# Three input projections of a decoder trunk: one 512-column pass for the high and the low part of 256 weight columns

## The chip, the cores and the metric

The kernel runs on one core of a Trainium2 chip. The metric is the device time of one execution in microseconds, from the first to the last instruction and what lies around them; lower is better.

## What is computed

A causal decoder of four layers on 512 tokens of 1024 features, float32. Each layer adds a token mixer and then a conv-gated MLP, each behind an RMS norm:

```python
for i in range(4):
    h = rms_norm(x, norm_mix[i])
    y = (dilated_attention, mla_attention, diff_attention, swa_sink_attention)[i](h, ...)
    x = x + y
    x = x + conv_ffn(rms_norm(x, norm_ffn[i]), ...)
```

Mixers 0, 2 and 3 begin with a projection of h onto 9*512, 3*1024 and 1280 columns. The columns give queries, keys and values; queries and keys are RMS-normed per head of 64 columns, the values are used as they are. Mixer 1 goes through two low-rank latents instead.

## The kernel before

**Precision.** Each float32 operand of the large products is split into a high part, rounded to the fp32r type of TensorE, and a low part, the rest. `mm3` (L304) makes a product of three matmuls: high by high, high by low, low by high. All three go into the same accumulator in PSUM.

**Layout.** The state is feature-major: `xh[k]`, `xl[k]` are the high and low part of features 128k to 128k+127, as 128 x 512 tokens. The projections of mixers 0, 2 and 3 are token-major: `tok` (L808) holds 128 tokens of `xh` or `xl` in the array (the weight load) and streams 256 columns of the projection's weights past them (the matmul). One call makes two token blocks c0 and c0+1, which share one PSUM bank of 512 columns, over k = 0 to 7: per k and block three loads and three matmuls of 256 columns.

**Units.** 256 weight columns are a unit: two weight tiles of 1024 columns (k 0 to 3, k 4 to 7), two calls of `tok`. Mixer 0 has 18 units (`ORDER0`), mixer 2 has 12, mixer 3 has 5. Behind each `tok` a task is spawned: `qk_post`, `q_post`, `kv_post` (squares, mean, normalising by `head_norm`, L831, all of which read the bank) or `v_post` (scaling by the row's norm factor). The bank is given back (`drop`, L828) when the task has read it. The tasks wait until the norm factor `self.rs` is known.

**Weights.** `wload` (L247 on) brings a tile from HBM into a ring of three, `_wsplit` (L233) makes the parts: ACT writes `wh` (L239), DVE writes `wl` (L242) of it. The parts stand in rings of three tiles each (`WB`, L67). `freew` (L265) gives a pair back; only then can the next item be split into it. In `tok` the first of a unit's two pairs goes back when the second call has used k = 3, so three quarters through the unit.

**Order.** The tasks are generators, of which each `round` (L123) runs one step. `tok` calls `round` once per k. The heads' work (logits, softmax, transposes, products with the values) is interleaved with the projections in this way. The instructions' order on each engine is then settled when the program is built, by a planner that goes by this order and by its own estimate of durations (`schedule_with_timeline_sim=True` in the launch lines); on the chip each engine runs its own list in order. PSUM has eight banks: three "a", two "lg", two "tr", one "av"; the projections use "a", and `self.early` (L976) lets the fourth and fifth call of a mixer use "lg".

Of the kernel before, what the change touches and what calls it, by code (L numbers as in the profile page):

```python
# [19 lines left out]
KD = 8  # L20
# [46 lines left out]
WB = 3  # L67
# [28 lines left out]
class Builder:  # L96
    def __init__(self, ctx, tc, ap, plan):
# [15 lines left out]
        self.ring(self.main, "wh", [128, WMAX], F32R, WB)  # L113
        self.ring(self.main, "wl", [128, WMAX], F32R, WB)
# [93 lines left out]
    def wpump(self):  # L208
        again = True
        while again:  # L210
# [13 lines left out]
            while self.wnext < len(self.witems) and self.free("wh") and self.free("wl"):  # L224
# [4 lines left out]
                wh, wl = self.now("wh"), self.now("wl")  # L229
                self.wsplit.append((wh, wl))  # L230
                self.spawn(self._wsplit(i, wh, wl))
# [33 lines left out]
    def freew(self):  # L265
        self.give("wh", "wl")
        self.wpump()
# [559 lines left out]

    def drop(self, bank):  # L828
        self.give(self.banks.pop(id(bank))[1])
# [144 lines left out]
    def mixer_rings(self, **more):  # L974
        mp = self.mp
        self.early = 5  # L976
# [21 lines left out]
    def mixer2(self):  # L998
# [8 lines left out]
        def qk_post(bank, c0, nt, h):  # L1007
            while self.rs is None:
                yield
            yield from self.head_norm([bank[:, i * 256:(i + 1) * 256] for i in range(2)],  # L1010
                                      [nt[:, c0 + i] for i in range(2)], 64,
                                      [self.e2[:, c0 + i:c0 + i + 1] for i in range(2)])
            self.drop(bank)
# [13 lines left out]
        def v_post(bank, c0, v, j):  # L1027
            while self.rs is None:
                yield
            for i in range(2):  # L1030
                nc.scalar.activation(v[:, c0 + i], bank[:, i * 256:(i + 1) * 256], AF.Copy,
                                     scale=self.rs[:, c0 + i:c0 + i + 1])
            self.drop(bank)
# [95 lines left out]
    def mixer0(self):  # L1129
# [11 lines left out]
        def qk_post(bank, c0, nt, p, g):  # L1141
            while self.rs is None:
                yield
            yield from self.head_norm([bank[:, i * 256:(i + 1) * 256] for i in range(2)],
                                      [nt[:, c0 + i] for i in range(2)], 64,
                                      [self.e2[:, c0 + i:c0 + i + 1] for i in range(2)])
            self.drop(bank)
# [16 lines left out]
        def v_post(bank, c0, v, store, key):  # L1164
            while self.rs is None:
                yield
            for i in range(2):
                nc.scalar.activation(v[:, c0 + i], bank[:, i * 256:(i + 1) * 256], AF.Copy,
                                     scale=self.rs[:, c0 + i:c0 + i + 1])
            self.drop(bank)  # L1170
# [149 lines left out]
        for p in range(4):  # L1320
            for t in ORDER0[p]:
                ws = [self.getw(), self.getw()]
                if t in (0, 1, 3):
                    x, g = self.now("nt"), (1, 2, None, 0)[t]
                    post = lambda b, c0: qk_post(b, c0, x, p, g)
                else:
                    y = self.now("v" if t == 4 else "vn")
                    post = lambda b, c0: v_post(b, c0, y, v0 if t == 4 else v12, p // 2 if t == 4 else p)
                for c0 in (0, 2):
                    b = self.tok(ws, 256, c0, self.xsrc, range(KD), done=c0 == 2)  # L1330
                    self.spawn(post(b, c0))
# [18 lines left out]
    def mixer1(self):  # L1350
        nc, mp = self.nc, self.mp
        self.mixer_rings(v=([128, 4, 256], F32, 2), nt=([128, 4, 384], F32, 2), p=([128, 512], F32, 10),
# [267 lines left out]
    def mixer3(self):  # L1620
# [9 lines left out]
        def kv_post(bank, c0, nt):  # L1630
            while self.rs is None:
                yield
            v = lambda i: bank[:, i * 256 + 128:(i + 1) * 256]
            for i in range(2):
                nc.scalar.activation(vh[:, c0 + i], v(i), AF.Copy, scale=self.rs[:, c0 + i:c0 + i + 1])
            yield from self.head_norm([bank[:, i * 256:i * 256 + 128] for i in range(2)],
                                      [nt[:, c0 + i, :128] for i in range(2)], 64,
# [297 lines left out]
```

## Time and profile before

| what | value |
|---|---|
| median of three runs | 2376.08 us (2373.54 to 2377.24) |
| the profiled execution | 2377.44 us |
| its span, first to last instruction | 2375.5 us |
| mean granted TensorE clock, share of full speed | 0.992 |
| TensorE busy | 98% of the span |
| DVE, ACT busy | 75%, 54% |

Busy times of TensorE are modelled to the end of each pipelined matmul, so neighbouring matmuls overlap in the records: a matmul of 256 columns shows as 283 to 289 ns, but the next begins 120 ns later. The time that a matmul takes is therefore read from a run of them in the chain of waits (length by count), not from its own duration.

### The profile page before, as it was taken

The numbers are of one execution on the slowest core, as the hardware profiler recorded it, in microseconds if no ns is written. First come the engines' busy times: TensorE is split into PE (matmuls) and PEld (weight loads), VectorE is DVE, ScalarE is ACT, GpSimd is POOL, SyncE is SP. The second block draws the span as 40 slices with busy tenths as digits, with TensorE's granted clock in tenths as the row PEclk, the third lists the DMA queues.
The fourth block names the chain that finished last, engine by engine and source line by source line (L and its number), as shares of the span: only waits on it lengthen the run. The fifth ranks groups of instructions, "written<-read, shape, count | busy, mean of one in ns | idle before, by whom it ended". The sixth has DMA issues, their size and how long they took to land.

```text
span 2375.5 us, 41007 instructions
## 1 busy us (share of the span) xinstructions
PE 2328.8 (98%) x16116; PEld 2116.3 (89%) x16116; DVE 1773.8 (75%) x3152; ACT 1279.8 (54%) x2378; POOL 310.6 (13%) x242
## 2 busy tenths in 40 slices
PE   8999989999999999999999999899999999999999
PEld 8999969999997777999989998799999977899998
DVE  6565688787768749877786776888787676987776
ACT  5565555544557746544554564554445575544443
POOL 0000022222002102212100000122220000222210
PEclk9999999999999999999999999899999999999999
DMA  5233255554231115655435554565542533655632
GB/s 182 82 99 90 90 138 166 150 150 136 76 104 45 34 58 153 176 151 152 123 93 153 147 143 130 145 164 152 149 138 74 144 101 93 176 161 152 160 107 89
DMA packets 98160, 298.43 MB, mean 126 GB/s; under 512 B 12144, under 2 KB 18480, under 8 KB 97968
## 3 DMA queue, kind: packets, MB, share of 16 engines
q1 hardware_dynamic: 85296, 249.67, 33.0%
q0 software_dynamic: 12672, 46.14, 11.0%
q8 instruction: 127, 2.08, 0.4%
q14 instruction: 65, 0.53, 0.1%
HBM read 273.62 MB, written 4.32 MB: 117 GB/s over the span
## 4 chain that ended last, share of the span: by engine, by line
PE 95%; DVE 3%; ACT 1%; issue 1%; DMA 0%; SPq 0%; DVEq 0%; ACTq 0%
PE a L302 51%; PE tr L302 19%; PE lg L302 17%; PE av L302 3%; PE tr L969 2%; PE tr L863 2%; DVE r L628 0%; DVE wl L242 0%; ACT p L284 0%; DVE p L909 0%; ACT wh L239 0%; DVE x L452 0%; DVE acc L466 0%; DMA x<-in_x_dram 0%; PE lg L1288 0%
## 5 line engine op out<-in xcount | busy, mean ns | idle before, releaser
L239 ACT ACTIVATE wh<-wraw 128x1024 fp32r<-128x1024 f32 (+3 forms) x357 | 357.8, 1007 | 486.6 <-PE a L302 214.8
L242 DVE TENSOR_TENSOR wl<-wraw,wh 128x1024 fp32r<-128x1024 f32 (+3 forms) x357 | 446.6, 1253 | 139.9 <-ACT wh L239 138.7
L302 PE MATMUL a<-wh,xh 128*128 128x256 f32 (+1 forms) x1088 | 313.7, 289 | 6.3 <-ACT xh L456 6.3
L302 PE MATMUL a<-wl,xh 128*128 128x256 f32 (+1 forms) x1088 | 311.4, 286 | 0.0
L302 PE MATMUL a<-wh,xl 128*128 128x256 f32 (+1 forms) x1088 | 310.4, 286 | 0.0
L302 PE MATMUL a<-ch,wh 128*128 128x256 f32 x960 | 271.6, 283 | 0.0
L302 PE MATMUL a<-cl,wh 128*128 128x256 f32 x960 | 271.5, 283 | 0.0
L302 PE MATMUL a<-ch,wl 128*128 128x256 f32 x960 | 271.4, 283 | 0.0
L302 PE MATMUL tr<-hl,wh 128*128 128x512 f32 x656 | 256.2, 390 | 0.0
L302 PE MATMUL tr<-hh,wh 128*128 128x512 f32 x656 | 255.6, 392 | 0.0
L302 PE MATMUL tr<-hh,wl 128*128 128x512 f32 x656 | 250.4, 390 | 0.0
L256 POOL DMA_DIRECT2D fraw<-in_wup_dram x80 | 69.4, 870 | 1182.3 <-DMA fraw<-in_wup_dram 591.2
L302 PEld LDWEIGHTS a<-wh,xh 128*128 128x128 f32 x1088 | 208.7, 192 | 9.4 <-ACT xh L456 6.3
L302 PEld LDWEIGHTS a<-wl,xh 128*128 128x128 f32 x1088 | 208.9, 192 | 2.1 <-issue 0.9
L302 PEld LDWEIGHTS a<-wh,xl 128*128 128x128 f32 x1088 | 208.0, 192 | 2.3 <-issue 1.1
L302 PE MATMUL a<-xh,wh 128*128 128x256 f32 (+1 forms) x704 | 206.6, 293 | 2.3 <-ACT wh L239 2.3
L302 PE MATMUL a<-xh,wl 128*128 128x256 f32 (+1 forms) x704 | 206.0, 293 | 0.0
L302 PE MATMUL a<-xl,wh 128*128 128x256 f32 (+1 forms) x704 | 205.1, 293 | 0.0
L302 PEld LDWEIGHTS a<-cl,wh 128*128 128x128 f32 x960 | 183.9, 192 | 1.4
L302 PEld LDWEIGHTS a<-ch,wh 128*128 128x128 f32 x960 | 183.8, 191 | 1.4
L302 PEld LDWEIGHTS a<-ch,wl 128*128 128x128 f32 x960 | 183.9, 192 | 0.0
L302 PEld LDWEIGHTS tr<-hh,wl 128*128 128x128 f32 x656 | 123.3, 188 | 25.1
(274 smaller groups left out, 5879.3 us busy)
## 6 DMA issues: line engine op xcount, KB each, us to landing
wraw<-in_wup_dram SPq DMA_DIRECT2D x136, 512.0 KB, 3.3
fraw<-in_wup_dram SPq DMA_DIRECT2D x80, 512.0 KB, 3.4
fraw<-in_wup_dram POOLq DMA_DIRECT2D x80, 512.0 KB, 5.8
wraw<-in_w_dram SPq DMA_DIRECT2D x69, 512.0 KB, 3.5
wraw<-in_wd_dram SPq DMA_DIRECT2D x64, 512.0 KB, 3.3
wraw<-in_wd_dram SPq DMA_DIRECT2D x32, 384.0 KB, 3.1
wraw<-in_o_dram SPq DMA_DIRECT2D x24, 384.0 KB, 3.3
sk<-qh SPq DMA_DIRECT2D x68, 128.0 KB, 2.4
```

The lines of the kernel that those rows point to most:

```text
L239: nc.scalar.activation(wh[:, sl], raw[:, sl], AF.Copy)
L242: nc.vector.tensor_tensor(wl[:, sl], raw[:, sl], wh[:, sl].bitcast(F32), op=OP.subtract)
L256: self.nc.gpsimd.dma_start(out=s["tile"][:, :s["n"]], in_=s["plus"], accum_op=OP.add)
L302: self.nc.tensor.matmul(out, a, b, start=start, stop=stop, skip_group_check=True)
L863: self.nc.tensor.transpose(b[:rows, o * 128:(o + 1) * 128], src(c), self.mirror if query else self.ident)
L969: nc.tensor.transpose(b[:, j * 128:(j + 1) * 128], blk, self.mirror)
```

## The change

`tok` is replaced, in mixers 0, 2 and 3, by `tok_wide`. A weight item is now one tile of two halves, high and low. One token block c at a time: per k one matmul of 512 columns, `xh` by high and low half side by side, into the two halves of a bank, and one of 256 columns, `xl` by the high half, added into the first half. The two halves are added outside PSUM by a new task `gather`: ACT copies the second half into the SBUF tile, DVE adds the first half to it, and the bank is given back. The later tasks read and overwrite the SBUF tile. `round` is called for every second k. The first weight tile of a unit goes back in the fourth block, seven eighths through the unit.

```diff
-        self.ring(self.main, "wh", [128, WMAX], F32R, WB)
-        self.ring(self.main, "wl", [128, WMAX], F32R, WB)
+        self.ring(self.main, "ww", [128, 2, WMAX], F32R, WB)
...
+    def tok_wide(self, ws, x, post):
+        per = KD // len(ws)
+        n = []
+
+        def gather(bank, out):
+            self.nc.scalar.activation(out, bank[:, 256:], AF.Copy)
+            yield
+            self.nc.vector.tensor_tensor(out, bank[:, :256], out, op=OP.add)
+            self.give("a")
+            n.append(out)
+
+        def then(c0):
+            while len(n) < c0 + 2:
+                yield
+            yield from post(c0)
+        for c in range(4):
+            out = self.now("a")
+            sl = slice(c * 128, (c + 1) * 128)
+            for k in range(KD):
+                w = ws[k // per][2][:, :, k % per * 256:k % per * 256 + 256]
+                a = self.xsrc(k)
+                self.mm(out.rearrange("p (i d) -> p i d", i=2), a[0][:, sl], w, k == 0)
+                self.mm(out[:, :256], a[1][:, sl], w[:, 0], False, k == KD - 1)
+                if c == 3 and (k + 1) % per == 0:
+                    self.freew()
+                if k % 2:
+                    self.round()
+            self.spawn(gather(out, x[:, c]))
+            if c % 2:
+                self.spawn(then(c - 1))
...
     def mixer_rings(self, **more):
         mp = self.mp
-        self.early = 5
...
-        def v_post(bank, c0, v, j):
+        def v_post(c0, v, j):
             while self.rs is None:
                 yield
             for i in range(2):
-                nc.scalar.activation(v[:, c0 + i], bank[:, i * 256:(i + 1) * 256], AF.Copy,
-                                     scale=self.rs[:, c0 + i:c0 + i + 1])
-            self.drop(bank)
+                nc.scalar.activation(v[:, c0 + i], v[:, c0 + i], AF.Copy, scale=self.rs[:, c0 + i:c0 + i + 1])
...
-                for c0 in (0, 2):
-                    b = self.tok(ws, 256, c0, self.xsrc, range(KD), done=c0 == 2)
-                    self.spawn(qk_post(b, c0, x, 2 * j + t - 1) if t else v_post(b, c0, x, j))
+                self.tok_wide(ws, x, lambda c0, t=t, j=j, x=x: qk_post(c0, x, 2 * j + t - 1) if t else v_post(c0, x, j))
```

`qk_post`, `q_post` and `kv_post` of the three mixers change in the same way, and mixer 1, which keeps `tok`, sets `self.early` itself.

## Rows read from the trace of the kernel before

**Rows 1.** The page: busy time (share of span) and count; chain by line
```profile
PE 2328.8 (98%) x16116; PEld 2116.3 (89%) x16116; DVE 1773.8 (75%) x3152; ACT 1279.8 (54%) x2378; POOL 310.6 (13%) x242
...
PE a L302 51%; PE tr L302 19%; PE lg L302 17%; PE av L302 3%; PE tr L969 2%; PE tr L863 2%; DVE r L628 0%; DVE wl L242 0%; ACT p L284 0%; DVE p L909 0%; ACT wh L239 0%; DVE x L452 0%; DVE acc L466 0%; DMA x<-in_x_dram 0%; PE lg L1288 0%
```

**Rows 2.** The three projection stretches: busy us and count per engine, granted clock, DMA
```profile
0.00:279.00 279.00, 272.71 (x2300) 258.16 (x2302) 168.62 (x489) 157.41 (x388) 8.88 (x15) 1.00 0.34 106
1255.00:1437.00 182.00, 181.61 (x1496) 179.74 (x1495) 123.37 (x359) 101.27 (x266) 0.00 (x0) 1.00 0.52 148
1858.00:1931.00 73.00, 73.00 (x608) 70.62 (x607) 48.41 (x156) 40.70 (x122) 0.00 (x0) 1.00 0.48 128
```

**Rows 3.** Chain of waits: start us, length us, engine, tile, line, count
```profile
1276.20 7.55 PE lg L302 x63
...
1542.04 5.76 PE a L302 x48
...
1571.75 4.56 PE tr L302 x20
...
1582.06 5.47 PE tr L302 x24
```

**Rows 4.** Groups by form, whole span: busy us, mean ns, idle before
```profile
L853 DVE TENSOR_TENSOR nt<-a,hst 128x256 f32<-128x256 f32 x88 | 33.2, 418 | 1.0
...
L840 ACT ACTIVATE sq<-a 128x256 f32<-128x256 f32 x88 | 28.6, 377 | 26.1 <-PE a L302 26.1
...
L1168 ACT ACTIVATE vn<-a,st 128x256 f32<-128x256 f32 x14 | 5.9, 463 | 4.4 <-PE a L302 4.4
...
L627 DVE TENSOR_TENSOR r<-cv 128x256 f32<-128x256 f32 x16 | 6.7, 417 | 0.0
```

**Rows 5.** One stretch in mixer 3, columns as in rows 2
```profile
1905.00:1926.00 21.00, 21.00 (x179) 19.82 (x178) 17.88 (x65) 14.30 (x45) 0.00 (x0) 1.00 0.40 104
```

**Rows 6.** Timeline of ACT and DVE, mixer 2: a weight split that follows its release
```profile
1264.93 1.06 ACT L239 ACTIVATE wh<-wraw 128x1024 fp32r<-128x1024 f32 x1 [0.96 <-PE a L302]
...
1266.03 1.23 DVE L242 TENSOR_TENSOR wl<-wraw,wh 128x1024 fp32r<-128x1024 f32 x1 [0.66 <-ACT wh L239]
```

**Rows 7.** The same later: a split that has to queue on DVE
```profile
1324.83 1.06 ACT L239 ACTIVATE wh<-wraw 128x1024 fp32r<-128x1024 f32 x1 [0.29 <-PE a L302]
...
1324.66 1.94 DVE L1058 SCALAR_TENSOR_TENSOR p<-p,hs 128x512 f32<-128x512 f32 x4
...
1327.98 1.22 DVE L242 TENSOR_TENSOR wl<-wraw,wh 128x1024 fp32r<-128x1024 f32 x1
```

**Rows 8.** Chain of waits at the three mixers' ends, start and length us
```profile
304.75 0.70 DVE oa L1258
...
306.27 0.64 ACT oh L293
...
1489.10 0.61 ACT sq L840
...
1491.68 0.70 DVE ot L853
...
1937.46 0.39 DVE p L909
...
1939.38 0.40 DVE p L909
```

**Rows 9.** Start of the program: timeline of DVE, then ACT, where the input's parts are made
```profile
14.29 2.07 DVE L463 SCALAR_TENSOR_TENSOR xl<-x,cols,xh 128x512 fp32r<-128x512 f32 x3
...
12.75 1.94 ACT L456 ACTIVATE xh<-x,cols 128x512 fp32r<-128x512 f32 x3
```

More of the change, by code (lines that the diff above doesn't have):

```diff
@@ L223, in wpump @@
                 again = True
[L224 removed]
+            while self.wnext < len(self.witems) and self.free("ww"):
                 i = self.wnext
@@ L228, in wpump @@
                 self.wnext += 1
-                wh, wl = self.now("wh"), self.now("wl")
-                self.wsplit.append((wh, wl))
+                ww = self.now("ww")
+                wh, wl = ww[:, 0], ww[:, 1]
+                self.wsplit.append((wh, wl, ww))
                 self.spawn(self._wsplit(i, wh, wl))
@@ L1005, in mixer2, with qk_post @@
         half, qk, vs, odone = {}, {}, {}, [0] * 8
-        def qk_post(bank, c0, nt, h):
+        def qk_post(c0, nt, h):
             while self.rs is None:
                 yield
-            yield from self.head_norm([bank[:, i * 256:(i + 1) * 256] for i in range(2)],
-                                      [nt[:, c0 + i] for i in range(2)], 64,
+            yield from self.head_norm(*[[nt[:, c0 + i] for i in range(2)]] * 2, 64,
                                       [self.e2[:, c0 + i:c0 + i + 1] for i in range(2)])
-            self.drop(bank)
             half[h] = half.get(h, 0) + 1
@@ L1139, in mixer0, with qk_post @@
         rem = lambda t: t.rearrange("p (r i) -> p r i", r=4)
-        def qk_post(bank, c0, nt, p, g):
+        def qk_post(c0, nt, p, g):
             while self.rs is None:
                 yield
-            yield from self.head_norm([bank[:, i * 256:(i + 1) * 256] for i in range(2)],
-                                      [nt[:, c0 + i] for i in range(2)], 64,
+            yield from self.head_norm(*[[nt[:, c0 + i] for i in range(2)]] * 2, 64,
                                       [self.e2[:, c0 + i:c0 + i + 1] for i in range(2)])
-            self.drop(bank)
             half[p, g] = half.get((p, g), 0) + 1
@@ L1162, in qk_post, with v_post @@
                 qk[p, g] = parts
-        def v_post(bank, c0, v, store, key):
+        def v_post(c0, v, store, key):
             while self.rs is None:
@@ L1323, in mixer0 @@
                 if t in (0, 1, 3):
-                    x, g = self.now("nt"), (1, 2, None, 0)[t]
-                    post = lambda b, c0: qk_post(b, c0, x, p, g)
-                else:
[L1327 to L1331, printed above, removed]
+                    x = self.now("nt")
+                    post = lambda c0, x=x, p=p, g=(1, 2, None, 0)[t]: qk_post(c0, x, p, g)
+                else:
+                    x = self.now("v" if t == 4 else "vn")
+                    post = lambda c0, x=x, p=p, t=t: v_post(c0, x, v0 if t == 4 else v12, p // 2 if t == 4 else p)
+                self.tok_wide(ws, x, post)
         def osrc(i):
@@ L1650, in kv_post, with q_post @@
                 half["k"] = True
-        def q_post(bank, c0, nt, t):
-            yield from self.head_norm([bank[:, i * 256:(i + 1) * 256] for i in range(2)],
-                                      [nt[:, c0 + i] for i in range(2)], 64,
+        def q_post(c0, nt, t):
+            while self.rs is None:
+                yield
+            yield from self.head_norm(*[[nt[:, c0 + i] for i in range(2)]] * 2, 64,
                                       [self.e2[:, c0 + i:c0 + i + 1] for i in range(2)])
-            self.drop(bank)
             half[t] = half.get(t, 0) + 1
@@ L1722, in mixer3 @@
             ws = [self.getw(), self.getw()]
-            for c0 in (0, 2):
-                b = self.tok(ws, 256, c0, self.xsrc, range(KD), done=c0 == 2)
-                self.spawn(kv_post(b, c0, nt) if t < 0 else q_post(b, c0, nt, t))
+            self.tok_wide(ws, nt, lambda c0, t=t, nt=nt: kv_post(c0, nt) if t < 0 else q_post(c0, nt, t))
         def osrc(i):
```

17 lines of the change are left out of this document (6 added, 11 removed).

## The prediction

> **What bounds the kernel now.** I read the page first, then the chain of waits by line, then the busy time by stretch, and last a few runs of matmuls one by one. The page and the chain say TensorE: 98% busy, and nearly all of the chain is matmul lines, DVE's and ACT's shares rounding to nothing [rows 1]. A busy share made of modelled, overlapping records would not prove it, so the reader should look at the spacing in the chain. A run of 63 matmuls of 256 columns in mixer 2's projections takes 7.55 us, 119.8 ns each; a run of 48 in an MLP takes 5.76 us, 120 ns each; 44 of 512 columns take 4.56 + 5.47 us, 228 ns each [rows 3]. The spacing in the projections is that of the undisturbed MLP, so they run at TensorE's own rate, and a stretch is made shorter only by giving TensorE less to do. The three stretches that the change touches are 279, 182 and 73 us long at a granted clock of 1.00 (the level of 2.4 GHz), with DVE busy for 60, 68 and 66% of them and ACT for 56, 56 and 56% [rows 2].
>
> **The saving.** 256 columns cost 120 ns and 512 cost 228, so 256 more columns cost 108, and some 12 ns are paid per load and matmul whatever its length [rows 3]. The change streams as many columns as before but in two passes where there were three: 228 + 120 = 348 ns in place of 3 x 120 = 360. There are 18 + 12 + 5 = 35 units of four token blocks and eight k, 1120 triples; 1120 x 12 ns = 13.4 us. All of it lies on the path. The trace shows no streamed operand in two pieces (the high and the low half lie 4 KB apart). Its bounds are the 228 ns of one piece, and 240, that is two separate passes and a saving of nought; a loss below that is excluded only if the joint costs less than a pass of its own, which I assume. I take 228, since the columns in each piece are 256 in a row.
>
> The Trainium skill ("TensorE: Matmul & The Clock Gate", Back-to-back issue gap) speaks against the change: it gives the warm gap as the columns at 2.4 GHz and about 2.5 ns more. By that a triple would save 2.5 ns and the whole 2.8 us. The trace does not agree: the rows have 12 ns, and the rows decide.
>
> **The gather.** Each of the 140 blocks gets an ACT copy of 128x256 out of PSUM and a DVE addition of the same size. Nearest rows: a square of that shape 377 ns, a scaled copy 463; the normalising product 418 [rows 4]. So 53 to 65 us on ACT and 59 us on DVE, none of it TensorE's. It lies beside the matmuls: with 72, 48 and 20 blocks in the three mixers, DVE goes to (168.6 + 30) of 272 us, (123.4 + 20) of 177 and (48.4 + 8.4) of 71, that is 73, 81 and 80%; ACT to about 68% in each [rows 2]. No mean reaches 100%. One stretch does: 21 us in mixer 3 where DVE is busy 17.9 us already [rows 5]; seven blocks end in it, 2.9 us more, 20.8 of 21. I charge 1 us for it (0 to 3), the part that cannot be caught up before mixer 3's heads finish. That squares and products now read SBUF costs nothing: 418 ns from PSUM, 417 from SBUF on DVE [rows 4].
>
> **The banks.** A bank is now held for its copy and addition, under 1 us, not through the head norm. Since TensorE didn't wait for banks in these stretches (spacing above), this gives nothing; nor does the loss of two "lg" banks at a mixer's start cost anything, as the gather needs no norm factor. Where copy or addition queue, two other banks cover 2 x 2.78 us of matmuls.
>
> **The weight tiles.** This is the step that costs. With a ring of three, a unit's second tile can be split only when the unit before gives back its first tile. Before, between that moment and the tile's first use, stood 24 + 24 matmuls, 5.76 us; now k = 4 to 7 of the last block and k = 0 to 3 of the next unit's first, 8 pairs, 8 x 0.348 = 2.78 us. And the first matmul now needs the low half too. In between ACT's and DVE's split must fit: in mixer 2 one runs from 1264.93 to 1267.26, 2.33 us, both engines taking it up at once [rows 6]. So there is cover, 0.45 us of it where no other matmuls stand between. Mostly they do: the 1728, 1152 and 480 projection matmuls of 120 ns are 207, 138 and 58 us of 279, 182 and 73 [rows 2], three quarters, so the mean cover is 2.78 / 0.76 = 3.7 us. Against it: a later split in mixer 2 queued behind DVE's work and took from 1324.83 to 1329.20, 4.37 us [rows 7], 0.7 us too long. Of 32 such transitions between units I let three be like that: 2 us. The bounds are 0 (all as rows 6) and 32 x 0.67 = 21 us (all as rows 7). ACT and DVE run their lists in order, so behind a late split stand the next blocks' copies and additions, and behind those the heads' softmax. I take a value near the lower bound because the planner puts other blocks' matmuls in front of a tile that it expects late.
>
> **The ends and the start.** A mixer's last heads begin one copy, one addition and two hand-overs later, 0.38 + 0.42 + 0.2 = 1.0 us. There TensorE does wait: in mixer 0 for the chain that ends in two additions and a copy from 304.75 on, in mixer 2 for one from 1489.10 to 1492.4, in mixer 3 for softmax on DVE [rows 8]. I charge 1 us each, 3 us (0 if the output projection's matmuls fill it, 6 if a DMA or a queue slips as well). At the program's start x's parts appear until 14.7 (high) and 16.4 us (low) [rows 9]; one block has only a third of the former matmuls per k ready in time, but three banks are open and later blocks' matmuls can go ahead: 0 (0 to 2 us).
>
> **Sum.** -13.4 + 2 (weights) + 3 (ends) + 1 (DVE in mixer 3) = -7.4 us. The profiled execution took 2377.44 us, of it 2375.5 span, and is 1.4 us over the median, inside the runs' spread of 3.7 us; the saving is the same off either. From the median: 2376.1 - 7.4 = 2368.7 us, 0.31% faster.
>
> **Rivals.** (a) *Full saving*: weights and ends cost nothing, 2376.1 - 13.4 = 2362.7. For it: rows 6, and that TensorE is nowhere idle in the stretches. Against it: chains at the ends that hold TensorE up already. (b) *Most of it given back at the ends and the transitions*: twice the ends (6 us), five or six late tiles (4), 1 in mixer 3, -13.4 + 11 = -2.4, 2373.7: no change that can be seen. For it: DVE at 80%, and that shorter projections leave the heads' latency as it is. (c) *Slower, by the weight tiles*: at each transition one copy and one addition of the gather stand ahead of the split, 2.33 + 0.2 (release) + 0.38 + 0.42 = 3.3 us against 2.78 without other matmuls; 0.54 us short 32 times is 17 us, and -13.4 + 17 + 4 = +8, 2384. It decides from a mean shortage of 13.4 / 32 = 0.42 us on, or 0.3 with the ends' 4 us. For it: TensorE runs its list in order, and the cover is halved. Against it: three quarters of that cover's time only is projection, and in rows 6 nothing stood ahead. (d) *The wide pass saves nothing*: two pieces cost two passes, 0 + 6 = +6, 2382. For it: no such operand in the trace; against it: 228 ns for 512 columns. (e) *A fixed cost of a few ns only*, so that the 12 ns belong to something that stays (the weight load, say): a gain of 3 us less 6 of costs, +3, 2379. Against it: the spacing grows by 108 ns for 256 columns and the change takes away a load as well. This is the outcome by the page named above.
>
> **How the numbers follow.** Forecast 0.48 (its own range 2365 to 2371), (a) 0.12, (b) 0.22, (c) 0.10, (d) 0.05, (e) 0.03. The range takes in (a), the forecast, (b) and (e): 2361.5 to 2380. A difference of 0.2% (4.8 us) is about what a measurement of this kernel can tell from none. Faster by more: the forecast and (a), 0.60. Within: (b), (e), 0.25. Slower: (c), (d), 0.15.
>
> **What would show it.** In the changed kernel's chain a run of the projections' pairs should be spaced 348 ns per pair; 360 or more means (d). Idle time of TensorE ended by ACT or DVE writing the weight tile, in front of the wide matmul, should sum to some 2 us; 15 us means (c). The stretch of mixer 0 should end some 5 to 7 us earlier, that of mixer 2 some 3 to 5. At the mixers' ends the idle time in front of the output projection should grow by about 1 us each. The prediction is wrong if the planner's new order shifts stalls at the ends or at the MLP's start by more than the few microseconds saved, which no row here can bound.

## The result: 12 us slower, and the profile after

| | before | after |
|---|---|---|
| median, measured side by side | 2376.65 us | 2388.99 us (2388.52 to 2390.50) |
| after / before | | 1.0053, 95% interval 1.0041 to 1.0066 |
| span of the profiled execution | 2375.5 us | 2387.2 us |

The prediction was 2368.7 us, with a range up to 2380. The change made the kernel slower, by 0.5%.

The page of the changed kernel: busy time by engine and the chain's shares by engine; behind them the chain's shares of the kernel before:

```profile
PE 2324.1 (97%) x14996; PEld 2056.5 (86%) x14996; DVE 1845.4 (77%) x3292; ACT 1329.9 (56%) x2518; POOL 307.7 (13%) x242
...
PE 89%; DVE 6%; issue 2%; ACT 1%; DMA 1%; SPq 0%; POOL 0%; DVEq 0%; POOLq 0%
```

```profile
PE 95%; DVE 3%; ACT 1%; issue 1%; DMA 0%; SPq 0%; DVEq 0%; ACTq 0%
```

1120 matmuls are gone, and TensorE's busy time has hardly moved. In the chain TensorE has lost six points and DVE won three: more of the span now hangs on other engines. To see where, I cut both spans at the same marks: a mixer's *stretch* runs from the last matmul that reads the MLP's hidden units (tiles `hh`, `hl`) to the mixer's last projection matmul, its *end* from there to the first matmul of the next MLP on `ch`. Each number is a difference of two starts in the trace (the MLPs' with the 4.2 us behind the last one):

| us | before | after | difference |
|---|---|---|---|
| mixer 0, stretch + end | 272.2 + 73.7 = 345.9 | 266.6 + 76.6 = 343.2 | -2.7 |
| mixer 1 | 264.4 | 264.1 | -0.3 |
| mixer 2, stretch + end | 180.9 + 103.0 = 283.9 | 180.0 + 113.5 = 293.5 | +9.6 |
| mixer 3, stretch + end | 72.2 + 121.8 = 194.0 | 78.0 + 117.8 = 195.8 | +1.8 |
| four MLPs | 1281.0 | 1284.6 | +3.6 |

That is +12.0; the first matmul starts 0.6 us earlier, and the spans differ by 11.7. Three quarters is mixer 2, nearly all of it at its end. The waits of TensorE there, first before, then after (engine, tile and line, who it waited for, us, times, longest):

```profile
PE tr L863 <- DVE ot L853: 3.6, 2, 3.4
PE lg L302 <- ACT wh L239: 3.6, 1, 3.6
```

```profile
PE tr L896 <- DVE ot L886: 10.5, 2, 7.1
PE lg L302 <- DVE ww L242: 6.0, 1, 6.0
```

The 6.0 us one stands in front of the next MLP's first matmul, which now needs both parts of its weight tile. It is not the loss: it is 5.8 us in the run ww_only below, whose mixer 2 takes 283.2 us. The 7.1 us one, in the timelines of TensorE and of DVE of the changed kernel (start, us, engine, line, what):

```profile
1449.14 0.83 PE L302 MATMUL av<-v,ptf 128*128 128x128 f32 x6
1457.11 1.12 PE L896 MATMUL tr<-ident,ot 128*128 128x128 f32 x4 [7.14 <-DVE ot L886]
```

```profile
1451.19 0.48 DVE L1085 TENSOR_SCALAR p<-p,hs 128x512 f32<-128x512 f32 x1
1451.60 0.68 DVE L876 TENSOR_REDUCE hst<-sq 128x4 f32<-128x512 f32 x1
1452.19 0.87 DVE L1085 TENSOR_SCALAR p<-p,hs 128x384 f32<-128x384 f32 x3
1452.98 0.74 DVE L1086 SCALAR_TENSOR_TENSOR p<-p,hs 128x512 f32<-128x512 f32 x1
...
1456.36 0.69 DVE L886 TENSOR_TENSOR ot<-av,hst 128x512 f32<-128x512 f32 x1
```

Head 5's products with the values are done at 1450, its output norm (L876 to L886) comes out at 1457, with head 6's combination (L1085, L1086) between its steps in DVE's list, and TensorE has no other work left in front of it: the projections ended at 1433.6. The heads are later than before, measured against the projections: head 5's norm writes `ot` at 1456.4 in place of 1447.3, though the projections end 2.3 us earlier.

The wait is paid a second time. Windows around it (length; busy us of TensorE, its weight loads, DVE, ACT, GpSimd; granted clock, DMA share, GB/s):

```profile
1446.00:1449.60 3.60, 3.60 (x31) 3.39 (x30) 0.50 (x3) 1.28 (x6) 0.00 (x0) 1.00 0.00 0
1449.60:1456.90 7.30, 0.37 (x4) 0.18 (x2) 6.42 (x24) 3.35 (x12) 0.00 (x0) 0.67 0.26 72
1456.90:1460.00 3.10, 2.89 (x10) 2.41 (x11) 1.83 (x5) 1.28 (x2) 0.00 (x0) 0.50 0.00 0
1460.00:1464.00 4.00, 4.00 (x20) 3.35 (x19) 2.17 (x4) 2.29 (x4) 0.00 (x0) 0.72 0.70 162
1464.00:1468.00 4.00, 3.50 (x16) 2.48 (x15) 3.41 (x5) 1.57 (x3) 0.00 (x0) 1.00 0.86 201
```

After 7 us with hardly a matmul the granted clock is 0.50, the level of 1.2 GHz; from 1464 on it is 1.00 throughout. 3.1 us at 0.50 and 4.0 us with a mean of 0.72 (4.0 x 0.28 / 0.5 = 2.2 us of it at the lower level) are 5.3 us at half rate, so an estimated 2.7 us more. Matmuls of 512 columns show both rates, the first two starting 0.43 us apart, the last two 0.23:

```profile
1461.73 0.63 PE L302 MATMUL a<-oh,ww 128*128 128x512 f32 x1
1462.16 0.45 PE L302 MATMUL a<-ol,ww 128*128 128x512 f32 x1
1462.45 0.40 PE L302 MATMUL a<-oh,ww 128*128 128x512 f32 x1
1462.68 0.39 PE L302 MATMUL a<-ol,ww 128*128 128x512 f32 x1
```

The Trainium skill ("TensorE: Matmul & The Clock Gate", HAM oscillation) describes this pattern behind waits for DMA: the work restarts at the lower level, and half of the time spent there is lost. The trace agrees, though TensorE waited here for DVE.

### The profile page after: what moved, and what is told of

Its sections match the earlier page's. It is cut to its first block, busy times and chain, and to the rows that moved or that the text cites. A ratio compares the mean times of both kernels' runs of the same rounds, so it can differ in the third digit from the quotient of the medians.

```text
span 2387.2 us, 39037 instructions
## 1 busy us (share of the span) xinstructions
PE 2324.1 (97%) x14996; PEld 2056.5 (86%) x14996; DVE 1845.4 (77%) x3292; ACT 1329.9 (56%) x2518; POOL 307.7 (13%) x242
## 4 chain that ended last, share of the span: by engine, by line
PE 89%; DVE 6%; issue 2%; ACT 1%; DMA 1%; SPq 0%; POOL 0%; DVEq 0%; POOLq 0%
PE a L302 49%; PE tr L302 19%; PE lg L302 15%; PE av L302 3%; PE tr L1002 2%; PE tr L896 2%; DVE ww L242 1%; DVE x L452 1%; DVE xl L463 1%; DVE acc L466 1%; DVE r L628 1%; ACT ptf L994 0%; ACT p L284 0%; DMA cols<-in_cols_dram 0%; DVE cl L295 0%
## 5 line engine op out<-in xcount | busy, mean ns | idle before, releaser
L239 ACT ACTIVATE ww<-wraw 128x1024 fp32r<-128x1024 f32 (+3 forms) x357 | 357.8, 1007 | 440.1 <-PE a L302 171.1
L242 DVE TENSOR_TENSOR ww<-wraw,ww 128x1024 fp32r<-128x1024 f32 (+3 forms) x357 | 450.5, 1266 | 112.9 <-ACT ww L239 111.8
L302 PE MATMUL a<-ww,xh 128*128 128x512 f32 (+2 forms) x1248 | 428.3, 391 | 6.0 <-ACT xh L456 5.7
L302 PE MATMUL tr<-hh,ww 128*128 128x512 f32 x1312 | 420.8, 391 | 1.5 <-DVE ww L242 1.3
L302 PE MATMUL a<-ch,ww 128*128 128x256 f32 x1920 | 364.9, 283 | 0.2
L302 PE MATMUL a<-ww,xl 128*128 128x256 f32 (+1 forms) x1184 | 333.0, 284 | 0.0
L302 PEld LDWEIGHTS a<-ch,ww 128*128 128x128 f32 x1920 | 307.4, 191 | 2.2 <-issue 0.9
L302 PE MATMUL a<-xh,ww 128*128 128x256 f32 (+1 forms) x1408 | 287.6, 293 | 0.0
L302 PE MATMUL a<-cl,ww 128*128 128x256 f32 x960 | 271.4, 283 | 0.0
L302 PE MATMUL tr<-hl,ww 128*128 128x512 f32 x656 | 256.2, 390 | 0.0
L302 PE MATMUL lg<-xh,ww 128*128 128x256 f32 (+1 forms) x768 | 170.4, 311 | 20.9 <-DVE ww L242 20.9
```

The costliest lines, as they stand in the source:

```text
L239: nc.scalar.activation(wh[:, sl], raw[:, sl], AF.Copy)
L242: nc.vector.tensor_tensor(wl[:, sl], raw[:, sl], wh[:, sl].bitcast(F32), op=OP.subtract)
L302: self.nc.tensor.matmul(out, a, b, start=start, stop=stop, skip_group_check=True)
```

## The experiments

Executions of one kernel spread over 2 to 7 us, in three cases over some 8 to 9, and a stage table comes from one of them. How much of that is in a stage can be read from kernels whose instructions stand in the same order on TensorE, DVE and ACT: mixer 0 is the same, one by one, in after, after_ownsq, no_m2, contig and hold and takes 341.3 to 344.2 us; mixer 2 is the same in ww_only and no_m2 and takes 283.2 and 285.7. So a stage shows differences from some 3 us on, and a cause is better read from several kernels with the same stage. The last column is a measure of how the heads stand in TensorE's list of mixer 2: from the start of DVE's last combination of a head (L1086, L1058 before) to its first transpose on TensorE (`tr` by `mirror` and `p`), summed over the eight heads. A ratio is against the kernel before, run beside it.

| run | median us | ratio (95%) | mixer 0 | mixer 2 | mixer 3 | MLPs | heads wait in list |
|---|---|---|---|---|---|---|---|
| before | | | 345.9 | 283.9 | 194.0 | 1281.0 | 20.3 |
| after | 2388.99 | 1.0053 (1.0041 to 1.0066) | 343.2 | 293.5 | 195.8 | 1284.6 | 31.4 |
| ww_only | 2380.04 | 1.0012 (1.0003 to 1.0022) | 345.9 | 283.2 | 194.5 | 1284.6 | 20.7 |
| load_only | 2385.26 | 1.0034 (1.0021 to 1.0047) | 349.1 | 288.2 | 192.6 | 1281.0 | 21.1 |
| no_add | 2383.43 | 1.0025 (1.0014 to 1.0035) | 342.7 | 293.3 | 191.3 | 1284.6 | 35.2 |
| pool_add | 2381.83 | 1.0021 (1.0012 to 1.0030) | 343.4 | 290.8 | 191.3 | 1284.6 | 38.3 |
| inline | 2384.31 | 1.0024 (1.0015 to 1.0034) | 346.6 | 290.9 | 191.5 | 1284.6 | 32.8 |
| after_ownsq | 2386.14 | 1.0034 (1.0021 to 1.0047) | 341.6 | 292.7 | 195.1 | 1284.6 | 26.4 |
| before_ownsq | 2377.99 | 1.0003 (0.9993 to 1.0012) | 346.0 | 286.9 | 194.2 | 1281.2 | 16.4 |
| no_m2 | 2379.56 | 1.0007 (0.9997 to 1.0016) | 341.3 | 285.7 | 193.6 | 1284.6 | 21.2 |
| order_only | 2384.17 | 1.0029 (1.0019 to 1.0039) | 350.8 | 284.6 | 194.7 | 1282.0 | 20.9 |
| copy_dve | 2384.99 | 1.0030 (1.0018 to 1.0043) | 342.8 | 294.3 | 191.4 | 1284.6 | 38.3 |
| contig | 2388.69 | 1.0046 (1.0030 to 1.0062) | 344.2 | 293.5 | 195.8 | 1284.6 | 31.3 |
| best | 2376.01 | 0.9993 (0.9984 to 1.0002) | 345.2 | 284.9 | 192.0 | 1286.3 | 21.3 |
| hold | 2384.15 | 1.0030 (1.0020 to 1.0039) | 343.2 | 289.4 | 195.0 | 1284.6 | 29.9 |
| early_rel | 2377.75 | 0.9998 (0.9988 to 1.0007) | 347.1 | 285.0 | 194.0 | 1280.8 | 24.0 |
| hold_pool | 2386.30 | 1.0031 (1.0019 to 1.0043) | 342.4 | 294.8 | 190.8 | 1284.7 | 43.7 |
| narrow | 2389.90 | 1.0052 (1.0037 to 1.0067) | 353.2 | 286.9 | 194.0 | 1284.6 | 23.4 |
| rounds | 2435.35 | 1.0239 (1.0222 to 1.0256) | 346.2 | 320.7 | 212.1 | 1284.6 | 25.3 |
| low_first | 2388.05 | 1.0045 (1.0028 to 1.0062) | 340.9 | 293.4 | 195.8 | 1284.6 | 32.3 |

Mixer 1, which no run edits, takes 263.6 to 265.1 us but for order_only (260.5) and best (260.8).

The first theories: W, the joint weight tile costs the MLPs; L, the gather's load on ACT and DVE makes the heads late; H, the hand-over of the new tasks does; O, the order that the planner makes of it; C, the odd heads hang on each other through the ring of squares.

**ww_only: the joint tile alone**, in the kernel before.

```diff
-        self.ring(self.main, "wh", [128, WMAX], F32R, WB)
-        self.ring(self.main, "wl", [128, WMAX], F32R, WB)
+        self.ring(self.main, "ww", [128, 2, WMAX], F32R, WB)
```

> The kernel before, with one edit: high and low part of a weight item share one tile, so that a slot comes free only when both parts are used up. Theory W (the joint tile costs the MLPs about 1 us each, 4 in all, through its later release): 2379 to 2381 us, with TensorE waiting about 0.6 us for DVE's weight part in each MLP, as in the changed kernel. Rival: the MLPs' loss comes with the rest of the change: 2376 us, 0.2 us of such waits.

The four MLPs take 3.6 us more, as in the changed kernel, and the mixers nothing. Where a weight tile comes late, the first matmul, which needs the high half, now waits for DVE's low half too. In the changed kernel, at the end of the first MLP:

```profile
649.78 0.73 PE L302 MATMUL tr<-hh,ww 128*128 128x512 f32 x2 [0.44 <-DVE ww L242]
```

Before, no wait is recorded here. The same wait of 0.44 us stands in the first three MLPs, which are 0.9 to 1.1 us longer each; the fourth is 0.7 us longer without one. So W stands, though these waits are only part of its price.

**load_only: the gather's load alone**, in the kernel before.

```diff
+    def extra(self):
+        for i in range(2):
+            g = yield from self.take("gs")
+            self.nc.scalar.activation(g, self.x[0][:, :256], AF.Copy)
+            yield
+            self.nc.vector.tensor_tensor(g, self.x[0][:, :256], g, op=OP.add)
+            self.give("gs")
...
                     b = self.tok(ws, 256, c0, self.xsrc, range(KD), done=c0 == 2)
+                    self.spawn(self.extra())
```

> The kernel before, with the gather's work added and nothing else: behind each projection call two ACT copies and two DVE additions of 128x256 on SBUF, for whose result nobody waits (280 more instructions, 53 us on ACT and 58 on DVE). Theory L (the loss is DVE's and ACT's extra time, which makes the heads late): 2384 to 2392 us, mixer 2's end 5 us or more longer. Rival H (the loss is the hand-over, later tasks waiting for copy and addition): 2376 to 2379. Rival O (the loss is the order that the planner made of it): either, but not in the same places.

Load that nobody waits for costs 8 us in all, 4.3 in mixer 2 and 3.2 in mixer 0. It is no free cover.

**no_add, pool_add, copy_dve: parts of the gather taken away.**

```diff
-            self.nc.scalar.activation(out, bank[:, 256:], AF.Copy)
+            self.nc.scalar.activation(out, bank[:, :256], AF.Copy)   # no_add
             yield
-            self.nc.vector.tensor_tensor(out, bank[:, :256], out, op=OP.add)
...
+            self.nc.scalar.activation(g, bank[:, 256:], AF.Copy)     # pool_add
+            self.nc.scalar.activation(out, bank[:, :256], AF.Copy)
+            self.nc.gpsimd.tensor_tensor(out, out, g, op=OP.add)
...
+            self.nc.vector.tensor_copy(out, bank[:, :256])           # copy_dve
```

> The changed kernel without the addition: the gather is one ACT copy of the first half of the bank, so the product of the input's high part with the weights' low part is left out of the result. TensorE's work, the weight tiles and one of the two hand-overs stay. Theory L: most of the loss goes, 2370 to 2378 us. Rival H: about half of it stays, 2380 to 2384. Rival O: anywhere between 2370 and 2395, with the waits at other places.

> The changed kernel with the addition on GpSimd, which is idle in these mixers: ACT copies both halves out of PSUM (two copies of 128x256), GpSimd adds them. DVE has 58 us less than in the changed kernel, ACT some 53 us more, the chain is one copy longer. Theory L, if DVE is the engine: 2372 to 2381 us. If ACT is: 2389 or more. Rival H (hand-over): 2390 to 2395.

> The changed kernel with a gather of one DVE copy of the bank's first half: ACT's copy and the addition are gone, so the product of the high part of the input with the low part of the weights is left out of the projections. Beside the earlier run in which ACT's copy alone was kept, this asks which engine's list carries the delay. If the copies that stand in ACT's list hold up the heads of mixer 2, mixer 2 falls from 293 us to 288 or less and the median is 2378 to 2381. If it is the order of the blocks, mixer 2 stays at 291 to 294 and the median at 2382 to 2386.

Mixer 3 falls by 4.4 to 4.5 us in all three: there the gather is the loss. Since copy_dve gives DVE as many operations as the changed kernel does and gains as much, it is not DVE's load. What DVE waited for in mixer 3's stretch of the changed kernel, and the stretch as a window, then the window with the addition on GpSimd:

```profile
DVE nt L837 <- ACT nt L835: 6.7, 9, 3.8
```

```profile
1867.30:1945.30 78.00, 75.59 (x458) 64.24 (x456) 57.06 (x184) 49.97 (x148) 0.00 (x0) 0.98 0.44 120
```

```profile
1864.80:1933.30 68.50, 67.61 (x413) 58.30 (x413) 49.27 (x139) 46.73 (x143) 15.34 (x18) 1.00 0.46 125
```

The two stretches do not hold the same work (458 and 413 matmuls, as the heads' share differs), so only stretch and end together can be compared. DVE is 73% busy (57.06 of 78.00), so not full; but it stood 6.7 us in front of additions whose copy ACT had not made, with the heads' work behind them in its list. That standing alone is not the loss either. In the next run, inline, copies and additions are all there, DVE stands in front of them for longer, and mixer 3 takes 191.5 us:

```profile
DVE nt L836 <- ACT nt L835: 7.7, 9, 3.8
```

That points to where the gather's steps and what waits for them come to stand in the lists; which of them costs the 4.4 us is not shown. In mixer 2 none of the three gives more than 2.7 us, about the spread. Each of them leaves an operation or two per block, and load_only cost 4.3 us there, so these three alone do not refute L; the run narrow below bears on it too.

**inline: no hand-over.** Copy and addition are issued at the block's end, without tasks of their own.

```diff
-            self.spawn(gather(out, x[:, c]))
+            gather(out, x[:, c])
             if c % 2:
-                self.spawn(then(c - 1))
+                self.spawn(post(c - 1))
```

> The changed kernel with copy and addition issued at the end of each block's matmuls, not by a task one and two rounds later, and the later task spawned at once. Same instructions. Rival H (the loss is the hand-over by tasks): mixer 2 5 us or more shorter, 2379 to 2384 us. Theory C: the chain is passed in the same way, 2386 to 2390.

Mixer 2 gets 2.6 us shorter, mixer 0 3.4 us longer. H is about a quarter of mixer 2's loss at most, and the 2.6 us are not clear of the spread.

**after_ownsq, before_ownsq: the ring of squares.** The squares of a head's output go into `ot`, not into `sq`.

```diff
-        sq = yield from self.take("sq")
+        sq = extra if extra is not None else (yield from self.take("sq"))
```

> The changed kernel, with one edit in mixer 2: the squares of a head's output go into the output's own tile, not into the ring of two square tiles that the projections' norms use too. Theory C (mixer 2's length is set by a chain in which a projection's squares stand behind the output's squares of the head two before, heads 1, 3, 5, 7; the ring ties them): mixer 2, from its first projection matmul to the MLP, 293.5 us in the changed kernel, falls by 5 us or more; the whole 2375 to 2384 us. Rival O (the order on ACT is the planner's choice and not tied by the ring): 2387 to 2391, the two squares still next to each other.

> The kernel before with the same one edit. Theory C: the chain is there before the change too; mixer 2 takes less than its 284 us, by 2 us or more, 2370 to 2375 us in all. Rival O: 2376 to 2379.

Mixer 2 takes 292.7 us in the first and 286.9 in the second, 3.0 more than before: no gain in either. C fell.

**no_m2: mixer 2 as before**, the change in mixers 0 and 3 only (`mixer2` of the kernel before, with the joint tile).

> The change in mixers 0 and 3 alone; mixer 2 has the projection calls of before (with the joint weight tile). Theory C: mixer 2 goes back to 283 to 284 us and the whole to 2377 to 2380 us, as nothing that mixer 2's projections gain reaches its end. Rival O: mixer 2 somewhere else in 280 to 294, by its new place behind a changed mixer.

Mixer 2 is back at 285.7: its loss is made in it, not inherited. **best** is this kernel with the gather's addition on GpSimd:

> The wide pass in mixers 0 and 3 only, mixer 2 as it was before (with the joint weight tile); in mixers 0 and 3 ACT copies both halves of the bank and GpSimd adds them, so that DVE has nothing of the gather. From the earlier runs' stages: mixer 0 342 us in place of 346, mixer 3 191.5 in place of 194, the four MLPs 3.5 us longer by the joint tile, mixer 2 within 2 us of before: -4 - 2.5 + 3.5 + 1 = -2, so a median 1 to 4 us under that of the kernel before. If mixer 2's length hangs on something else that the wide pass leaves behind, it is 2 us or more above.

2376.01 us, ratio 0.9993, with 1 in the interval: the best of these kernels is as fast as the kernel before, no more. Its stages did not come as expected: mixer 0 takes 345.2 us (342 expected) and the MLPs 5.3 more than before (3.5 expected), against 3.6 less in mixer 1, where the order is that of the changed kernel and TensorE's longest wait is 2.5 us in place of 4.4.

**order_only: the block order alone**, in the kernel before; and **contig: the two pieces side by side**, in the changed one.

```diff
-        for j, k in enumerate(ks):
+        for i, j in [(i, j) for i in range(cs) for j in range(len(ks))]:   # order_only
...
-                self.mm(out.rearrange("p (i d) -> p i d", i=2), a[0][:, sl], w, k == 0)
+                w = ws[k // per][2].rearrange("p i z -> p (i z)")[:, k % per * 512:k % per * 512 + 512]   # contig
+                self.mm(out, a[0][:, sl], w, k == 0)
```

> The kernel before, with nothing of the wide pass, the joint tile or the gather: the call that makes two token blocks runs all eight k of the first block, then all eight k of the second, in place of both blocks at each k; the scheduling round comes at every second k, and a unit's first weight tile goes back seven eighths through the unit. Theory O (the order of the blocks and the later release of the tiles are what delays mixer 2's heads): mixer 2, stretch and end together, grows by 5 us or more over the 284 us of before, and the median comes to 2381 or above. Theory L (the gather's work in ACT's and DVE's lists is what delays them): mixer 2 within 2 us of before and the median 2375 to 2379.

> The changed kernel with the projections' weight tile laid out so that high and low part of 256 columns stand side by side: the wide pass streams 512 columns in one piece, and nothing else is different. If the two pieces cost 4 to 5 ns, the pair of matmuls is spaced 346 to 348 ns in place of 351, TensorE has 5 us less to do in the three stretches, and mixer 0 gets 2 to 3 us shorter. If mixer 2's length is set by its heads and not by TensorE, mixer 2 stays within 1.5 us of 293.5. Median then 2384 to 2387; 2388 to 2390 if the pieces cost nothing.

The block order leaves mixer 2 alone and costs mixer 0 some 5 us. Its profiled execution was the shortest of nine (2380.2 us), so its stages understate it. Contiguous pieces change nothing; two runs of the pairs in the changed kernel's chain, then in contig's (start, us, engine, tile, line, count):

```profile
1269.27 7.06 PE a L302 x40
...
1325.61 9.01 PE a L302 x52
```

```profile
1270.40 7.06 PE a L309 x40
...
1326.75 9.02 PE a L309 x52
```

7.06 / 20 = 353 ns and 9.01 / 26 = 347 ns per pair, in both kernels. Over all pairs of the three mixers that stand between other projection matmuls (some 890) the mean distance from start to start is 350.4 ns, in contig 350.3; over such triples of the kernel before (some 850) it is 359.1.

**hold, early_rel, hold_pool: how long a bank is held** (theory B).

```diff
+    def keep(self, x, c0):                                           # hold
+        bank = self.banks.pop((id(x), c0))
+        t = yield from self.take("hst")
+        self.nc.vector.tensor_copy(t[:, :1], bank[:, :1])
+        self.give("hst", "a")
...
+        def copy(bank, c0, x):                                       # early_rel
+            nc.scalar.activation(x[:, c0:c0 + 2], bank.rearrange("p (i d) -> p i d", i=2), AF.Copy)
+            self.drop(bank)
```

> The changed kernel; in mixer 2 alone one bank of each pair of blocks is kept until the head norm (or the value scaling) of the pair is done, where a DVE copy of one column reads it once more and gives it back, so that as many banks are held as long as before the change. Theory B (banks that come free at once let the planner put projections ahead of the heads' work in TensorE's list, and the heads' tail then lies behind the last projection): mixer 2 comes back to 284 to 288 us, with its projections ending later relative to the heads, and the median is 2380 to 2383. Rival F (the shorter, faster projections themselves leave less to hide the heads' latency): mixer 2 stays at 291 to 295, median 2386 to 2390. Keeping banks may also hold TensorE up: then waits in the stretch grow by more than 5 us.

> The kernel before with three narrow matmuls and separate weight tiles as they were; in mixer 2 alone each bank is copied by ACT as a whole (128x512) into the SBUF tile as soon as its two blocks are done and given back, and the head norm and the value scaling read SBUF. Theory B: mixer 2 grows from 284 to 289 to 294 us though TensorE's work is that of before, and the median is 2381 to 2386. Rival F: mixer 2 stays within 2 us of 284, median 2376 to 2379. ACT gets 24 copies of some 0.6 us more; if that is what counts, mixer 2 grows too, by up to the 4 us of the earlier run with idle copies and additions, but its projections do not run ahead of the heads.

> The run hold with the gather of all three mixers as in the earlier run with the addition on GpSimd (ACT copies both halves, so the bank of the pair's first block is free after two copies). By theory B and the earlier stages: mixer 2 284 to 288, mixer 3 191.5, mixer 0 343.4, the four MLPs 3.5 us over before: -3 - 2.5 + 2 + 3.5 = 0, median 2374 to 2379. By rival F mixer 2 stays at 291 and the median is 2381 to 2384.

early_rel decides: banks that come free at once leave mixer 2 at 285.0, also with the head norms reading SBUF. hold gains 4 us, and the same hold with the gather on GpSimd loses 4 (290.8 to 294.8). B fell.

**rounds: a round at every k.** `if k % 2:` ahead of `self.round()` is taken out.

> The changed kernel with a scheduling round at every k of the wide projection in place of every second k, in all three mixers: the heads' steps are put among half as many projection matmuls, so they come earlier in the order that the planner starts from. If the heads of mixer 2 are late because they stand too far back in TensorE's, ACT's and DVE's lists, the mixer falls to 284 to 288 us and the median to 2380 to 2383. If it is work or latency and not place, mixer 2 stays within 2 us of 293, or TensorE waits inside the stretch for heads that come too early, and the median is 2386 to 2392.

2435 us: mixer 2 grows by 27 us and mixer 3 by 16, the stretches by 15 and 3 of these. Both expectations missed. No work was added; how the heads' steps are woven among the projections is worth tens of microseconds, and earlier is not better.

**narrow: the wide pass taken back out.** Gather, joint tile, block order and tasks stay.

```diff
-                self.mm(out.rearrange("p (i d) -> p i d", i=2), a[0][:, sl], w, k == 0)
+                self.mm(out[:, :256], a[0][:, sl], w[:, 0], k == 0)
+                self.mm(out[:, 256:], a[0][:, sl], w[:, 1])
```

> The changed kernel in all but the wide pass: its 512 columns are two matmuls of 256, so a triple is three loads and three matmuls as before the change (360 ns), and the gather, the joint tile, the block order and the later tasks stay. Rival F (the wide pass leaves less projection time to hide the heads): mixer 2's waits of TensorE fall back to 16 to 20 us and the mixer takes 284 to 288 us; mixer 0 3 us longer than in the changed kernel; median 2381 to 2385. Theory G (the gather's tasks delay the heads whatever the matmuls): mixer 2 grows by the 3 to 4 us of matmul time to 295 to 298 and the median is 2392 to 2396, the whole of the wide pass's saving on top of the changed kernel.

Mixer 2 is back at 286.9, as F said, and mixer 0 is 10 us longer. So in mixer 0 the wide pass brings more than its 576 x 8.8 ns = 5.1 us, and in mixer 2 it costs 6.6 us. F's reason, less time to hide the heads, covers only the 384 x 8.8 ns = 3.4 us of matmuls that came back. The run bears on L, H and G in mixer 2 as well: it carries the whole gather with all its tasks and is only 3.0 us over the kernel before, so none of them makes the 9.6 us by itself.

**low_first: the same narrow matmuls, the low half first**, in mixer 2; and two more banks at mixer 0's start.

```diff
-                self.mm(out[:, :256], a[0][:, sl], w[:, 0], k == 0)
-                self.mm(out[:, 256:], a[0][:, sl], w[:, 1])
+                self.mm(out[:, 256:], a[0][:, sl], w[:, 1], k == 0)
+                self.mm(out[:, :256], a[0][:, sl], w[:, 0])
...
+            tag = "lg" if 1 <= self.early <= 2 else "a"
+            out = self.now(tag)
```

> Two edits of the changed kernel in two separate stages. In mixer 2 the wide pass is again two matmuls of 256 columns as in the run narrow, but the one with the weights' low half stands first of each triple, ahead of the one with the high half: the same matmuls, as many, as long. Theory D (what the first matmul of a triple waits for decides where the projection comes to stand among the heads' work): mixer 2 takes 289 to 293 us, against 286.9 in narrow. Rival F (the time under which the heads are hidden decides): 286 to 288 as in narrow. In mixer 0 the fourth and fifth block may use the two other PSUM banks, as before the change: if the start of the program is what costs mixer 0 its extra 3 us of waits, its first unit ends near 19.6 us in place of 22.9 and the mixer takes 340 us in place of 343; if not, nothing changes there. Median 2381 to 2386 by D with the start, 2378 to 2382 by F with it.

Mixer 2 takes 293.4 us, as with the wide pass, and with TensorE's work as in narrow. Its end in narrow and in low_first, as windows, and the waits of TensorE in it:

```profile
1445.20:1550.00 104.80, 92.49 (x469) 77.14 (x468) 78.24 (x161) 53.80 (x106) 12.84 (x8) 0.95 0.47 133
...
PE tr L897 <- DVE ot L887: 3.7, 1, 3.7
```

```profile
1433.30:1545.10 111.80, 95.45 (x470) 79.73 (x468) 78.91 (x163) 54.32 (x107) 14.65 (x8) 0.91 0.45 127
...
PE tr L902 <- DVE hst L323: 5.4, 1, 5.4
PE tr L902 <- DVE ot L892: 3.4, 1, 3.4
```

In mixer 2 two neighbouring matmuls have changed places in each triple, nothing else; the end's mean clock and its waits for a head's norm are again those of the slow kernels. Ahead of it the two kernels differ too, as narrow has the narrow matmuls in mixer 0. But that doesn't reach mixer 2's order, as ww_only and no_m2 show: there mixer 0 differs and mixer 2's lists are the same, one by one. In narrow and low_first mixer 2 has the same operations in another order, on TensorE, DVE and ACT. So F is refuted as well: it is neither the time nor the length of the wide pass, but the order that the lists get. That the low half's later arrival is what moves it, as D says, fits (the wide pass needs the low half at once, narrow does not); but the swap also changes which half of the bank is begun first, and no run separates the two.

What sets mixer 2's length is the same in all twenty kernels: from the start of DVE's write of the last head's norm (`ot`) to the mixer's end it is 46 to 48 us in each. That write in the changed kernel, in narrow and in low_first (before: [rows 8]):

```profile
1499.04 0.69 DVE L886 TENSOR_TENSOR ot<-av,hst 128x512 f32<-128x512 f32 x1
...
1503.41 0.69 DVE L887 TENSOR_TENSOR ot<-av,hst 128x512 f32<-128x512 f32 x1 [0.46 <-DVE hst L324]
...
1497.06 0.69 DVE L892 TENSOR_TENSOR ot<-av,hst 128x512 f32<-128x512 f32 x1
```

From the start of mixer 2's stretch these are 245.5, 240.2 and 245.4 us; before it was 236.7, in rounds 272.8.

The last column of the table is a sign of it and no cause. In all kernels whose mixer 2 takes 283 to 288 us the heads' first transposes come 16 to 24 us behind the combination, summed; in those with 289 to 295 us it is 26 to 44; but in rounds, the slowest by far, it is 25. The second head of the kernel before and of the one after, DVE's combination and TensorE's transposes:

```profile
1324.66 1.94 DVE L1058 SCALAR_TENSOR_TENSOR p<-p,hs 128x512 f32<-128x512 f32 x4
...
1331.74 0.60 PE L969 MATMUL tr<-mirror,p 128*128 128x128 f32 x4
```

```profile
1325.11 1.93 DVE L1086 SCALAR_TENSOR_TENSOR p<-p,hs 128x512 f32<-128x512 f32 x4
...
1335.37 0.60 PE L1002 MATMUL tr<-mirror,p 128*128 128x128 f32 x4
```

The work is ready at 1326.6 and 1327.0 and starts 5.1 and 8.3 us later, behind projection pairs. TensorE doesn't idle there, so no list of waits shows it. Counting heads from 0, the norms of heads 1, 3, 5 and 7 write `ot` at 1344.7, 1394.0, 1447.3 and 1491.7 before, and 5.5, 8.2, 9.1 and 7.3 us later after the change. That head 5's delay, the 7.1 us wait, is handed down from head 1 does not follow. By the measure of the table head 1 waits 8.8 us in the changed kernel, and also 8.7 in narrow, 8.6 in early_rel and 8.1 in order_only, whose mixer 2 takes 284.6 to 286.9 us. And from narrow to low_first, counted from the stretch's start, the norms of heads 0 to 4 move by no more than 3.2 us either way, while head 5's comes 5.2 us later. Why the planner's order puts it there stays open.

**The start**, in low_first. Windows of before, after and low_first:

```profile
12.00:20.00 8.00, 8.00 (x69) 8.00 (x68) 7.91 (x20) 6.15 (x10) 0.00 (x0) 1.00 0.83 285
```

```profile
12.00:20.00 8.00, 6.95 (x34) 4.40 (x32) 7.91 (x23) 6.13 (x13) 0.00 (x0) 1.00 0.83 280
```

```profile
12.00:20.00 8.00, 8.00 (x45) 6.26 (x43) 7.92 (x20) 7.19 (x14) 0.00 (x0) 1.00 0.80 267
```

With one block to a bank and three banks, TensorE runs out of work while the input arrives; the first unit's last matmul starts at 22.9 us in place of 19.6. With five banks it starts at 19.0. Of these 3.9 us the last unit of mixer 0 has 1.0 left, and the mixer takes 340.9 us, in place of 341.3 to 344.2 in the five kernels with the order of the changed one: a gain that is not clear of the spread. These banks are not in the kernel best.

## Why the prediction was wrong, point by point

**The saving** (-13.4) was mis-sized, its place partly right: mixer 0's stretch is 5.6 us shorter (5 to 7 forecast), mixer 2's 0.9 (3 to 5 forecast), and of that nothing reached mixer 2's end. A pair takes 350.4 ns in the mean, not 348, and a triple took 359.1, not 360: 1120 x 8.8 ns = 9.8 us. The two pieces, the only unknown that I had bounded, are innocent: contig has 350.3. Why some runs of pairs have 347 ns and others 353 stays open. The Trainium skill's figure ("TensorE: Matmul & The Clock Gate", Back-to-back issue gap), 2.5 ns a pass, would make it an estimated 2.8 us; the measurement lies between that and the forecast.

**The weight tiles** (+2, and the 17 us of rival (c)): no wait of TensorE for a weight tile stands in the three stretches of the changed kernel, so this term was nought. What I left out is the joint tile where the change saves nothing: 3.6 us in the four MLPs, shown by ww_only.

**The gather.** Its prices were right: 376 ns for ACT's copy, 418 for DVE's addition. That reading SBUF costs nothing was read off DVE alone: ACT's square takes 412 ns from SBUF, against 377 from PSUM before [rows 4]:

```profile
L873 ACT ACTIVATE sq<-nt 128x256 f32<-128x256 f32 x96 | 38.4, 412 | 26.5 <-DVE nt L837 26.3
```

"No mean reaches 100%" was the wrong question. Mixer 3 pays 4.4 us for the gather, against 1 charged, at 73% of DVE; as inline gets these back with all copies and additions in place, they do not come from the sum of its work.

**The start** (0, up to 2): the first unit is 3.3 us late (22.9 in place of 19.6). What of it is left at mixer 0's end, 2.3 us by low_first, is within the spread. I counted banks and forgot that a bank now holds one block in place of two.

**The ends** (1 us each) was the step that failed. I let a mixer's last heads begin one copy, one addition and two hand-overs later, and took the order of everything else as given. Mixer 2's end grew by 10.5 us, mixer 0's by 2.9, mixer 3's shrank by 4.0 while its stretch grew by 5.8. Taking away the copy, the addition or the hand-over returned at most 2.7 us of mixer 2's loss; swapping two equal matmuls moved 6.5. So what failed is the overlap that I took as unchanged: in the new order of the lists the last head's norm came 8.8 us later, counted from the stretch's start, and the mixer's end with it. The last sentence of my working had named it, a new order of the planner that no row can bound, and given it no term and no share of the chances. Rival (b) had the place, the ends, but charged 2 us a mixer where mixer 2's grew by 10.5; rival (c) had the sign and the wrong mechanism.

## What to carry to other kernels

When TensorE is 98% busy and its order is planned beforehand, saved matmul time is only a gain where the next thing is matmuls; where a chain through other engines sets a stage's end, as mixer 2's heads do, it need not shorten the stage, and here edits of what the hidden work waits for re-dealt the order by several microseconds either way. Put that re-deal into the range, some 10 us here, before summing nanoseconds. And look for it in the time at which the stage's last chain is done (here the last head's norm), since an engine that is busy with the wrong work shows no wait.

## What was unexpected of the hardware

Streaming 512 columns in two pieces 4 KB apart costs nothing against one piece: a pair of matmuls of 512 and 256 columns is spaced 350.4 ns in the first case and 350.3 in the second, near the sum of the spacings of 512 alone (228) and 256 alone (120). ACT's square of 128x256 takes 412 ns from SBUF and 377 from PSUM. A wait of 7.1 us was followed by 5.3 us at the 1.2 GHz level, an estimated 2.7 us on top of the wait.
